# Batched matmul of transposed operands: next batch's transposes, as words of two bf16, ahead of this batch's matmuls; b loaded four rows to a partition; stores three batches behind

## The chip, the cores and the metric

The kernel runs on one core of a Trainium2 chip. The metric is the device time of one execution in microseconds (us); lower is better. A core has a matrix engine (TensorE, PE in the profile, with its weight loads listed apart as PEld), a vector engine (VectorE, DVE), a scalar engine (ScalarE, ACT), a general engine (GpSimd, POOL) and a synchronisation engine (SyncE, SP) from whose queue this kernel starts its transfers. Sixteen DMA engines move the data between the main memory and the core's working memory, which has 128 partitions. The matrix engine writes to a separate accumulator memory (PSUM).

## The reference

There are 16 independent products. Both operands arrive transposed: a is stored as k by m, b as n by k.

```python
batch, m, k, n = 16, 512, 512, 512
a: (batch, k, m) float32      b: (batch, n, k) float32
np.matmul(a.transpose(0, 2, 1), b.transpose(0, 2, 1)).astype(np.float32)
```

So `out[i][m][n]` is the sum over k of `a[i][k][m] * b[i][n][k]`. Each batch reads 1 MiB of a and 1 MiB of b and writes 1 MiB of output; over 16 batches that is 33.55 MB read and 16.78 MB written.

## The kernel before, in words

The matrix engine contracts over the partitions, so k must lie on the partitions in both operands. a has k as its rows already: partition ki takes the four rows k = 4 ki + rk (rk from 0 to 3), one run of 8 KB. b has n as its rows and must be transposed on the chip. Its view puts row n = 128 no + ni on partition ni, so that a partition takes four runs of 2 KB from four places (`b_v`, "b (no ni) k -> b ni no k").

One loop runs over the batches, and all of a batch's work stands in it in order:

- two loads from SP's queue, b first (L54), then a (L56), into pools of three buffers each;
- four casts of a to bf16 on ACT, each 128 by 512 (L60);
- for each rk, four transposes of 128 by 128 fp32 blocks on PE (L68; k is taken in steps of four elements, so that it matches a's order) into one PSUM bank, and a copy of that bank by DVE (L73) that turns it into bf16 and writes it to `bt_sb`;
- for each of four residues rm of the output rows, four matmuls of 128 by 128 by 512 that accumulate over rk in one PSUM bank (L80), and an eviction into `o_sb`, by ACT for even rm (L88) and by DVE for odd rm (L90);
- the store of the batch LAG = 6 earlier (L50, called at L93), again from SP's queue. The last six stores follow behind the loop (L96).

Each engine takes its instructions in this written order, and the waits between engines and for free buffers are put in by the tile framework. Nothing is planned apart from that. An instruction at the head of SP's queue that must wait, for a buffer to come free or for an eviction, therefore holds the transfers written behind it. There are four PSUM banks for transposes and four for outputs, and eight output buffers.

Of the kernel before, what the change touches and what calls it, by code (L numbers as in the profile page):

```python
# [1 line left out]

# [5 lines left out]


@with_exitstack
def kernel(
    ctx: ExitStack,
    tc: tile.TileContext,
    a: bass.AP,
    b: bass.AP,
    out: bass.AP,
):
    nc = tc.nc
    P = 128  # L20
    B, K, M = a.shape
    _, N, _ = b.shape
    KO = K // P
    MO = M // P
    NO = N // P

    f32 = mybir.dt.float32
    cdt = mybir.dt.bfloat16

    a_v = a.rearrange("b (ki ko) m -> b ki ko m", ko=KO)  # L30
    b_v = b.rearrange("b (no ni) k -> b ni no k", ni=P)
    out_v = out.rearrange("b (mi mo) n -> b mi mo n", mo=MO)

    const = ctx.enter_context(tc.tile_pool(name="const", bufs=1))
    identity = const.tile([P, P], f32)
    make_identity(nc, identity)

    a_pool = ctx.enter_context(tc.tile_pool(name="a_pool", bufs=3))
    b_pool = ctx.enter_context(tc.tile_pool(name="b_pool", bufs=3))
    ac_pool = ctx.enter_context(tc.tile_pool(name="ac_pool", bufs=4))  # L40
    bt_pool = ctx.enter_context(tc.tile_pool(name="bt_pool", bufs=3))
    o_pool = ctx.enter_context(tc.tile_pool(name="o_pool", bufs=8))
    psum_t = ctx.enter_context(tc.tile_pool(name="psum_t", bufs=4, space=bass.MemoryType.PSUM))
    psum_o = ctx.enter_context(tc.tile_pool(name="psum_o", bufs=4, space=bass.MemoryType.PSUM))

    LAG = 6
    o_tiles = {}

    def emit_out_dma(j):
        nc.sync.dma_start(out_v[j], o_tiles.pop(j))  # L50

    for i in range(B):
        b_sb = b_pool.tile([P, NO, K], f32)
        nc.sync.dma_start(b_sb, b_v[i])  # L54
        a_sb = a_pool.tile([P, KO, M], f32)
        nc.sync.dma_start(a_sb, a_v[i])  # L56

        a_bf = ac_pool.tile([P, KO, M], cdt)
        for rk in range(KO):
            nc.scalar.copy(a_bf[:, rk, :], a_sb[:, rk, :])  # L60
        a_br = a_bf.rearrange("p rk (pm rm) -> p rk rm pm", rm=MO)

        b_sr = b_sb.rearrange("p no (pk rk) -> p no rk pk", rk=KO)
        bt_sb = bt_pool.tile([P, KO, N], cdt)
        for rk in range(KO):
            bt_ps = psum_t.tile([P, N], f32)
            for no in range(NO):
                nc.tensor.transpose(  # L68
                    bt_ps[:, no * P:(no + 1) * P],
                    b_sr[:, no, rk, :],  # L70
                    identity,
                )
            nc.vector.tensor_copy(bt_sb[:, rk, :], bt_ps)  # L73

        o_sb = o_pool.tile([P, MO, N], f32)
        o_tiles[i] = o_sb
        for rm in range(MO):
            o_ps = psum_o.tile([P, N], f32)
            for rk in range(KO):
                nc.tensor.matmul(  # L80
                    o_ps,
                    a_br[:, rk, rm, :],
                    bt_sb[:, rk, :],
                    start=(rk == 0),
                    stop=(rk == KO - 1),
                )
            if rm % 2 == 0:
                nc.scalar.copy(o_sb[:, rm, :], o_ps)  # L88
            else:
                nc.vector.tensor_copy(o_sb[:, rm, :], o_ps)  # L90

        if i >= LAG:
            emit_out_dma(i - LAG)  # L93

    for j in range(B - LAG, B):
        emit_out_dma(j)  # L96


# [1 line left out]
_INS = ['a', 'b']  # L100
_OUTS = [((16, 512, 512), 'float32')]


# [23 lines left out]
```

## Time and profile before

| What | Before |
|---|---|
| Time, median of 3 runs (lowest to highest) | 129.46 us (129.3 to 129.65) |
| Span of the profiled execution, first to last instruction | 127.8 us |
| Profiled execution's own device time | the profile gives its span only |
| PE busy / its weight loads | 92.5 us (72%) / 60.6 us (47%) |
| DVE busy | 61.5 us (48%) |
| ACT busy | 54.8 us (43%) |
| Transfers: bytes, mean rate | 50.42 MB, 394 GB/s |
| Largest groups by busy time | matmuls 59.0 us, DVE transposed copies 40.0 us, transposes 35.7 us, ACT casts 34.9 us |
| Median time from issue to landing, 1 MiB each | b 15.4 us, a 17.3 us, out 17.4 us |

Busy shares are of the span. The page also gives the span in 40 equal slices, with one digit per slice for the busy share of each engine (9 is 90% or more), and the granted clock of the matrix engine in the same way. A matmul's listed duration includes the time in which it overlaps its neighbours, so its pace is better read from start to start. Time to landing counts from the issue on SP and includes the time that the transfer queues behind earlier ones. A timeline line gives start, duration, engine, line and operation, and in brackets the idle time before it with what ended it.

### The profile page before, as it was taken

The numbers are of one execution on the slowest core, as the hardware profiler recorded it, in microseconds if no ns is written. First come the engines' busy times: TensorE is split into PE (matmuls) and PEld (weight loads), VectorE is DVE, ScalarE is ACT, GpSimd is POOL, SyncE is SP. The second block draws the span as 40 slices with busy tenths as digits, with TensorE's granted clock in tenths as the row PEclk, the third lists the DMA queues.
The fourth block names the chain that finished last, engine by engine and source line by source line (L and its number), as shares of the span: only waits on it lengthen the run. The fifth ranks groups of instructions, "written<-read, shape, count | busy, mean of one in ns | idle before, by whom it ended". The sixth has DMA issues, their size and how long they took to land.

```text
span 127.8 us, 1405 instructions
## 1 busy us (share of the span) xinstructions
PE 92.5 (72%) x504; PEld 60.6 (47%) x512; DVE 61.5 (48%) x96; ACT 54.8 (43%) x97; POOL 0.7 (1%) x6
## 2 busy tenths in 40 slices
PE   0099999999999995768767796877779777670000
PEld 0094858678586763364634536353364634430000
DVE  0053668586774865463544727355472635640000
ACT  4026747646674635407163460816337072540000
POOL 2000000000000000000000000000000000000000
PEclk9999999999999999999999999999999999998555
DMA  3999999999999999999999999999999999999980
GB/s 90 402 370 422 406 399 420 382 409 398 404 417 415 417 419 394 416 410 429 420 410 423 406 436 405 416 426 413 427 402 431 412 424 418 426 428 428 426 346 36
DMA packets 13063, 50.42 MB, mean 394 GB/s; under 512 B 768, under 2 KB 768, under 8 KB 8960
## 3 DMA queue, kind: packets, MB, share of 16 engines
q1 hardware_dynamic: 13056, 50.33, 97.5%
q8 instruction: 4, 0.07, 0.2%
q14 instruction: 3, 0.02, 0.0%
HBM read 33.55 MB, written 16.78 MB: 394 GB/s over the span
## 4 chain that ended last, share of the span: by engine, by line
DMA 50%; PE 34%; SPq 3%; ACT 1%; issue 1%; DVE 1%; ACTq 0%
DMA a_sb<-in_a_dram 32%; PE o_ps L80 22%; DMA out_dram<-o_sb 13%; PE bt_ps L68 12%; DMA b_sb<-in_b_dram 4%; SPq L56 3%; ACT a_bf L60 1%; DVE o_sb L90 1%; ACT o_sb L88 0%; ACTq L60 0%; SPq L50 0%
## 5 line engine op out<-in xcount | busy, mean ns | idle before, releaser
L80 PE MATMUL o_ps<-bt_sb,a_bf 128*128 128x512 bf16 x248 | 59.0, 385 | 9.1 <-ACT a_bf L60 8.7
L60 ACT CAST a_bf<-a_sb 128x512 bf16<-128x512 f32 x64 | 34.9, 615 | 39.6 <-DMA a_sb<-in_a_dram 39.5
L73 DVE CAST bt_sb<-bt_ps 128x512 bf16<-128x512 f32 x64 | 40.0, 683 | 14.7 <-PE bt_ps L68 14.7
L68 PE MATMUL bt_ps<-identity,b_sb 128*128 128x128 f32 x256 | 35.7, 295 | 12.8 <-DMA b_sb<-in_b_dram 12.8
L80 PEld LDWEIGHTS <-a_bf 128*128 128x128 bf16 x256 | 27.3, 115 | 35.8 <-ACT a_bf L60 17.7
L68 PEld LDWEIGHTS bt_ps<-identity,b_sb 128*128 128x128 f32 x256 | 33.9, 211 | 17.5 <-PE o_ps L80 8.5
L90 DVE COPY o_sb<-o_ps 128x512 f32<-128x512 f32 x32 | 22.1, 692 | 38.9 <-PE o_ps L80 21.9
L88 ACT COPY o_sb<-o_ps 128x512 f32<-128x512 f32 x32 | 18.8, 586 | 19.0 <-PE o_ps L80 18.9
L60 ACT ACT_TABLE_LOAD x1 | 1.3, 1283 | 0.7 <-PEq L111 0.7
masks.py:199 POOL TENSOR_SCALAR_AFFINE_SELECT identity<-identity 128x128 f32<-128x128 f32 x1 | 0.3, 292 | 0.1
masks.py:197 POOL MEMSET identity<- 128x128 f32 x1 | 0.2, 204 | 0.3 <-POOLq L111 0.3
L111 POOL MEMSET const-bfloat16-1.0<- 128x1 bf16 x1 | 0.1, 101 | 0.0
L111 POOL MEMSET const-uint8-127<- 128x1 uint8 x1 | 0.1, 101 | 0.0
L111 POOL MEMSET const-float32-0.0<- 128x1 f32 x1 | 0.1, 98 | 0.2 <-issue 0.2
L111 POOL MEMSET const-float32-1.0<- 128x1 f32 x1 | 0.1, 98 | 0.0
## 6 DMA issues: line engine op xcount, KB each, us to landing
b_sb<-in_b_dram SPq DMA_DIRECT2D x16, 1024.0 KB, 15.4
a_sb<-in_a_dram SPq DMA_DIRECT2D x16, 1024.0 KB, 17.3
out_dram<-o_sb SPq DMA_DIRECT2D x16, 1024.0 KB, 17.4
```

What stands on the lines that cost most here:

```text
L56: nc.sync.dma_start(a_sb, a_v[i])
L60: nc.scalar.copy(a_bf[:, rk, :], a_sb[:, rk, :])
L68: nc.tensor.transpose(bt_ps[:, no * P:(no + 1) * P], b_sr[:, no, rk, :], identity,)
L73: nc.vector.tensor_copy(bt_sb[:, rk, :], bt_ps)
L80: nc.tensor.matmul(o_ps, a_br[:, rk, rm, :], bt_sb[:, rk, :], start=(rk == 0), stop=(rk == KO - 1),)
L88: nc.scalar.copy(o_sb[:, rm, :], o_ps)
L90: nc.vector.tensor_copy(o_sb[:, rm, :], o_ps)
L111: nc = _bacc.Bacc("TRN2", target_bir_lowering=False, num_devices=1)
```

## The change

- **b's layout.** Row n = 4 ni + no goes to partition ni, so a partition takes four neighbouring rows, one run of 8 KB.
- **b is cast first.** DVE casts the whole b tile of a batch to bf16 in one instruction (128 by 2048). The result is looked at as fp32 words, each of which is a pair of bf16 with neighbouring k. Eight transposes of 128 by 128 words take the place of sixteen.
- **n put in order by the copies.** The columns come out of the transposes grouped by no; two DVE copies per batch write them to word position n = 4 ni + no, that is with a step of four words. The matmuls then read one half of each word: bf16 elements with a step of two.
- **a in two casts** on ACT, each 128 by 1024, in place of four.
- **Order.** The body is split in `load`, `prepare` and `multiply`. A pass of the loop loads and prepares batch i (casts, transposes, copies), then multiplies and evicts batch i - 1, then stores batch i - 4. LAG is 3; the last three stores follow behind the loop.
- **Buffers.** a and b four each in place of three, bf16 a three in place of four, two for the bf16 b, outputs six in place of eight.

```diff
-    b_v = b.rearrange("b (no ni) k -> b ni no k", ni=P)
+    b_v = b.rearrange("b (ni no) k -> b ni no k", no=NO)
...
-    LAG = 6
+    LAG = 3
...
-        for rk in range(KO):
-            nc.scalar.copy(a_bf[:, rk, :], a_sb[:, rk, :])
...
-        b_sr = b_sb.rearrange("p no (pk rk) -> p no rk pk", rk=KO)
-        bt_sb = bt_pool.tile([P, KO, N], cdt)
-        for rk in range(KO):
-            bt_ps = psum_t.tile([P, N], f32)
+        bc = bc_pool.tile([P, NO, K], cdt, name="bc")
+        nc.vector.tensor_copy(bc, b_sb)
+        bc_w = bc.bitcast(f32).rearrange("p no (pk j) -> p no j pk", j=KJ)
+        bt_sb = bt_pool.tile([P, KJ, N], f32, name="bt_sb")
+        bt_w = bt_sb.rearrange("p j (ni no) -> p j no ni", no=NO)
+        for j in range(KJ):
+            bt_ps = psum_t.tile([P, NO, P], f32, name="bt_ps")
             for no in range(NO):
-                nc.tensor.transpose(
-                    bt_ps[:, no * P:(no + 1) * P],
-                    b_sr[:, no, rk, :],
-                    identity,
-                )
-            nc.vector.tensor_copy(bt_sb[:, rk, :], bt_ps)
+                nc.tensor.transpose(bt_ps[:, no, :], bc_w[:, no, j, :], identity)
+            nc.vector.tensor_copy(bt_w[:, j, :, :], bt_ps)
+        b_use[i] = bt_sb.bitcast(cdt).rearrange("p j (n h) -> p j h n", h=2)
...
+        for h in range(2):
+            nc.scalar.copy(a_bf[:, 2 * h:2 * h + 2, :], a_sb[:, 2 * h:2 * h + 2, :])
...
-                    bt_sb[:, rk, :],
+                    bt_h[:, rk // 2, rk % 2, :],
...
+    for i in range(B + 1):
+        if i < B:
+            load(i)
+            prepare(i)
+        if i >= 1:
+            multiply(i - 1)
+        if i >= LAG + 1:
+            nc.sync.dma_start(out_v[i - 1 - LAG], o_tiles.pop(i - 1 - LAG))
     for j in range(B - LAG, B):
-        emit_out_dma(j)
+        nc.sync.dma_start(out_v[j], o_tiles.pop(j))
```

More of the change, by code (lines that the diff above doesn't have):

```diff
@@ L23 @@
     KO = K // P
+    KJ = KO // 2
     MO = M // P
@@ L36 @@
     make_identity(nc, identity)
-    a_pool = ctx.enter_context(tc.tile_pool(name="a_pool", bufs=3))
-    b_pool = ctx.enter_context(tc.tile_pool(name="b_pool", bufs=3))
-    ac_pool = ctx.enter_context(tc.tile_pool(name="ac_pool", bufs=4))
+    a_pool = ctx.enter_context(tc.tile_pool(name="a_pool", bufs=4))
+    b_pool = ctx.enter_context(tc.tile_pool(name="b_pool", bufs=4))
+    ac_pool = ctx.enter_context(tc.tile_pool(name="ac_pool", bufs=3))
+    bc_pool = ctx.enter_context(tc.tile_pool(name="bc_pool", bufs=2))
@@ L41 @@
     bt_pool = ctx.enter_context(tc.tile_pool(name="bt_pool", bufs=3))
-    o_pool = ctx.enter_context(tc.tile_pool(name="o_pool", bufs=8))
+    o_pool = ctx.enter_context(tc.tile_pool(name="o_pool", bufs=6))
     psum_t = ctx.enter_context(tc.tile_pool(name="psum_t", bufs=4, space=bass.MemoryType.PSUM))
     psum_o = ctx.enter_context(tc.tile_pool(name="psum_o", bufs=4, space=bass.MemoryType.PSUM))
-    LAG = 6
-    o_tiles = {}
-    def emit_out_dma(j):
-        nc.sync.dma_start(out_v[j], o_tiles.pop(j))
@@ L52, with load, prepare @@
-    for i in range(B):
-        b_sb = b_pool.tile([P, NO, K], f32)
+    LAG = 3
+    o_tiles, a_tiles, b_tiles, a_use, b_use = {}, {}, {}, {}, {}
+    def load(i):
+        b_tiles[i] = b_sb = b_pool.tile([P, NO, K], f32, name="b_sb")
         nc.sync.dma_start(b_sb, b_v[i])
-        a_sb = a_pool.tile([P, KO, M], f32)
+        a_tiles[i] = a_sb = a_pool.tile([P, KO, M], f32, name="a_sb")
         nc.sync.dma_start(a_sb, a_v[i])
-        a_bf = ac_pool.tile([P, KO, M], cdt)
-        for rk in range(KO):
-            nc.scalar.copy(a_bf[:, rk, :], a_sb[:, rk, :])
-        a_br = a_bf.rearrange("p rk (pm rm) -> p rk rm pm", rm=MO)
-        b_sr = b_sb.rearrange("p no (pk rk) -> p no rk pk", rk=KO)
-        bt_sb = bt_pool.tile([P, KO, N], cdt)
-        for rk in range(KO):
-            bt_ps = psum_t.tile([P, N], f32)
-            for no in range(NO):
-                nc.tensor.transpose(
-                    bt_ps[:, no * P:(no + 1) * P],
-                    b_sr[:, no, rk, :],
-                    identity,
-                )
-            nc.vector.tensor_copy(bt_sb[:, rk, :], bt_ps)
-        o_sb = o_pool.tile([P, MO, N], f32)
-        o_tiles[i] = o_sb
+    def prepare(i):
+        b_sb, a_sb = b_tiles.pop(i), a_tiles.pop(i)
+        bc = bc_pool.tile([P, NO, K], cdt, name="bc")
[5 more added lines that the diff above has]
+            bt_ps = psum_t.tile([P, NO, P], f32, name="bt_ps")
+            for no in range(NO):
+                nc.tensor.transpose(bt_ps[:, no, :], bc_w[:, no, j, :], identity)
+            nc.vector.tensor_copy(bt_w[:, j, :, :], bt_ps)
+        b_use[i] = bt_sb.bitcast(cdt).rearrange("p j (n h) -> p j h n", h=2)
+        a_bf = ac_pool.tile([P, KO, M], cdt, name="a_bf")
+        for h in range(2):
+            nc.scalar.copy(a_bf[:, 2 * h:2 * h + 2, :], a_sb[:, 2 * h:2 * h + 2, :])
+        a_use[i] = a_bf.rearrange("p rk (pm rm) -> p rk rm pm", rm=MO)
@@ L77, with multiply @@
+    def multiply(i):
+        a_br, bt_h = a_use.pop(i), b_use.pop(i)
+        o_tiles[i] = o_sb = o_pool.tile([P, MO, N], f32, name="o_sb")
         for rm in range(MO):
-            o_ps = psum_o.tile([P, N], f32)
+            o_ps = psum_o.tile([P, N], f32, name="o_ps")
             for rk in range(KO):
@@ L90 @@
                 nc.vector.tensor_copy(o_sb[:, rm, :], o_ps)
-        if i >= LAG:
-            emit_out_dma(i - LAG)
+    for i in range(B + 1):
[6 more added lines that the diff above has]
+            nc.sync.dma_start(out_v[i - 1 - LAG], o_tiles.pop(i - 1 - LAG))
     for j in range(B - LAG, B):
-        emit_out_dma(j)
+        nc.sync.dma_start(out_v[j], o_tiles.pop(j))
 _INS = ['a', 'b']
```

## The prediction

> **What bounds the kernel now.** I read the page's slices and DMA queues first, since they say whether any engine has to be fast at all.
>
> ```profile
> PE   0099999999999995768767796877779777670000
> ...
> DMA  3999999999999999999999999999999999999980
> ...
> q1 hardware_dynamic: 13056, 50.33, 97.5%
> ```
>
> The transfer engines are full from the second slice to the last but one; no compute engine is. What counts is how long 48 transfers of 1 MiB take in one first-in-first-out queue. To split that by kind I read the timeline of ACT and PE: an a cast that waited for its load dates that load's landing, and a transpose group that waited dates b's.
>
> ```profile
> 31.09 2.18 ACT L60 CAST a_bf<-a_sb 128x512 bf16<-128x512 f32 x4 [0.90 <-DMA a_sb<-in_a_dram]
> 36.25 2.18 ACT L60 CAST a_bf<-a_sb 128x512 bf16<-128x512 f32 x4 [0.69 <-DMA a_sb<-in_a_dram]
> ...
> 100.04 2.17 PE L68 MATMUL bt_ps<-identity,b_sb 128*128 128x128 f32 x16 [0.78 <-DMA b_sb<-in_b_dram]
> 102.45 2.18 ACT L60 CAST a_bf<-a_sb 128x512 bf16<-128x512 f32 x4 [3.43 <-DMA a_sb<-in_a_dram]
> 107.58 2.17 PE L68 MATMUL bt_ps<-identity,b_sb 128*128 128x128 f32 x16 [0.77 <-DMA b_sb<-in_b_dram]
> 110.00 2.18 ACT L60 CAST a_bf<-a_sb 128x512 bf16<-128x512 f32 x4 [3.43 <-DMA a_sb<-in_a_dram]
> 110.67 3.69 PE L80 MATMUL o_ps<-bt_sb,a_bf 128*128 128x512 bf16 x15 [0.92 <-ACT a_bf L60]
> ```
>
> In the steady part a batch is one store, one b, one a: 110.00 - 102.45 = 7.55 us. An a follows its b by 110.00 - 107.58 = 2.42 us. Where only loads run, a pair takes 36.25 - 31.09 = 5.16 us, so b takes about 2.72 there. For stores I read the windows of the end, where nothing else is left (columns: stretch, us, busy of PE, its weight loads, DVE, ACT, POOL, clock, DMA share, GB/s).
>
> ```profile
> 109.92:117.00 7.08, 3.64 (x15) 1.61 (x16) 2.29 (x4) 3.35 (x6) 0.00 (x0) 1.00 1.01 428
> 117.00:122.00 5.00, 0.00 (x0) 0.00 (x0) 0.00 (x0) 0.00 (x0) 0.00 (x0) 0.54 1.00 424
> 123.50:124.00 0.50, 0.00 (x0) 0.00 (x0) 0.00 (x0) 0.00 (x0) 0.00 (x0) 0.50 0.66 279
> ```
>
> A store at 424 to 428 GB/s takes 1.0486 MB / 0.426 = 2.46 us. So b takes 7.55 - 2.42 - 2.46 = 2.67 us: 0.25 more than a for the same bytes (0.30 by the load-only stretch). The difference between the two loads is their pieces:
>
> ```profile
> DMA packets 13063, 50.42 MB, mean 394 GB/s; under 512 B 768, under 2 KB 768, under 8 KB 8960
> ```
>
> The 8960 - 768 = 8192 pieces between 2 and 8 KB are b's rows (16 x 512); a and out move in 2048 pieces of 8 KB each. The last bytes move near 124.2, the span ends 3.6 us later.
>
> [...] here the last window holds such a drop: clock 0.54 over 117 to 122 puts it near 117.4, 3.0 us after the last matmul ended at 114.37.
>
> **The change, part by part.**
>
> *b in 8 KB pieces.* b's load becomes piece for piece what a's is: 128 runs of 8 KB. Price per load falls from 2.67-2.72 to 2.42, so 16 x 0.25 to 16 x 0.30 = 4.0 to 4.8 us; I take 0.27, so 4.3 us. Nothing hides it: the queue is the bound from 2.3 us on. [...] A new batch is 2.42 + 2.42 + 2.46 = 7.30 us.
>
> *Transposes of word pairs.* 8 transposes instead of 16. They stay fp32 128x128, at 2.17 / 16 = 0.136 each: 1.09 us. [...] DVE gets a cast of 128x2048, which this trace doesn't have[...]. I take 1.23. The PSUM copies fall from 4 to 2; their write steps 16 bytes, so between 0.69 (the row of the old copy is 683 ns) and twice that. DVE per batch: 1.23 + 2 x 0.69 + 2 x 0.69 = 4.0[...]. ACT casts a in two instructions of 1024; by the old row two of 512 cost 1.23, less one fixed part, so about 1.05 each: ACT 2.1 + 2 x 0.59 = 3.3 us. All this lies beside the transfers; if that cover were gone, the cast would cost 1.23 us a batch between b's landing and its transposes, and the eight transposes saved would give back 1.09.
>
> *Matmuls on pairs.* For PE's pace I take an early stretch of its timeline, where it waits for nothing:
>
> ```profile
> 16.07 3.62 PE L80 MATMUL o_ps<-bt_sb,a_bf 128*128 128x512 bf16 x15
> 19.52 2.07 PE L68 MATMUL bt_ps<-identity,b_sb 128*128 128x128 f32 x16
> ```
>
> From start to start, 16 matmuls take 19.52 - 16.07 = 3.45 us, 0.216 each (x15: a record is missing). After the change the moving operand steps 4 bytes. [...] I take no loss; the far end, half rate, is 0.432 each. PE per batch: 1.09 + 3.45 = 4.54 of 7.30.
>
> *The order.* Matmuls of i-1 stand behind the transposes of i on PE, evictions of i-1 behind the a cast of i on ACT and the b cast of i on DVE, and the store of i-4 behind b and a of i on SP. So a store k can be issued only once batch k+1 has landed: 4.4 us after a(k+1) (see the end below). SP's next loads b(k+5), a(k+5) queue behind it; their buffers (four each) are free by then. Behind a(k+1) the queue still holds S(k-3), b, a, S(k-2), b, a, S(k-1), b, a: nine transfers, about 22 us. A wait of 4.4 us is hidden by that, and would have to grow by 17 us to starve the engines. At the start four buffers let eight loads go out where six went; the queue is full with six (no slice after the first is short), so I count nothing. The o buffers (six) are not short either: store k is through about three batches before its buffer's next use.
>
> *The end.* Here the shorter lag shows. Put 0 at the landing of a15, where b15 landed at -2.42. DVE casts until -1.1, PE transposes until 0, then runs the 16 matmuls of 14 until 3.5; ACT casts a15 until 2.1 and evicts two; DVE's last eviction of 14 ends at 4.4, store 14 goes. Matmuls of 15 follow on PE, 3.5 to 7.0, last eviction at 7.85, store 15 is issued. Bytes: landing is seen about 1.0 us after the last byte (b0's 1.05 MB were through near 5.2 and PE was released at 6.2), and first bytes follow an issue by 1.5 (0.73 to about 2.3 for b0). S11 to S14 therefore run from -1.0 to 8.8, and store 15's bytes start at 9.4: the engines idle 0.6 us, where six stores in hand left no gap before. Between 0 (all a little quicker) and 2 us[...].
>
> Sum: 127.8 - 4.3 + 0.6 = 124.1 us of span. The median of the runs is 129.46, 1.66 above this span, for what lies around it; the change touches none of that, so 129.46 - 3.7 = **125.8 us**, with 124.9 to 126.8 from the ends of the two terms.
>
> **Rivals.**
>
> *A cold PE at the end.* PE now idles 7.30 - 4.54 = 2.76 us in one piece per batch, where it had gaps of 0.8 and 0.9. The trace shows a drop 3.0 us after the last matmul. If the last batch falls in such a spell, 8 transposes take 1.8 us (the first group ran at 3.66 / 16 = 0.229) and the first matmuls 0.43 each: store 15 comes 1.4 to 3.1 us later, the gap is 2.0 to 3.7 us: 126.9 to 128.9, say 128.0. Mid-run it is hidden (even 1.8 + 5.2 is under 7.30). Against it: 2.76 is under 3.0, and no spell of the steady part, with its own gaps, shows a clock under 1.00.
>
> *Pieces matter less.* If something other than b's pieces made 2.67 us,[...] Against it: the a load beside it, same bytes, same queue.
>
> *PE becomes the bound (slower).* If a moving operand of 4-byte steps is read at half rate, a batch is 16 x 0.432 + 1.09 = 8.0 us, above 7.30. It decides from 0.39 us per matmul. Start near 7.5, 16 batches to 135.5, last eviction 0.9, store 1.5 + 2.46, end 3.6: span 144, run 145.6. No strided moving bf16 operand in the trace speaks either way[...].
>
> **How the numbers follow.** Main case 0.69, cold end 0.14, small packet gain 0.06, PE bound 0.07, and 0.04 for another loss of over 4 us, such as a starved queue. 0.3% (0.4 us) is about what a measurement of this kernel tells from no change. Faster: the main case, nearly all of the cold end and most of the small gain, 0.87; same 0.03; slower 0.10. The range reaches from 124.6 (all engines at the a load's pace, no gap) to 128.2, through most of the cold end.
>
> **What would show it.** b waits and a waits 2.4 us apart, a batch of 7.3 us; pieces under 8 KB down to 768 and GB/s slices near 425 from the start; PE near 4.5 us per batch; a dip in the DMA share one store before the end. Wrong if the matmul row grows past 0.39 us apart, if DMA digits fall mid-run, or if b still takes 2.67.

## The result, and the profile after

The change made the kernel slower: 135.4 us median of 4 runs (134.95 to 135.63) against 129.38 us (129.2 to 129.65), a ratio of 1.0468 with a 95% interval of 1.0442 to 1.0494. The profiled execution spans 133.7 us against 127.8. The forecast was 125.8 us, with a range of 124.6 to 128.2.

The page of the kernel after, slices and transfers (a digit is the busy share of one fortieth of the span, some 3.3 us):

```profile
PE   0079799998749378393893937938379383765930
...
PEclk9999999999999968999689997799977999998698
DMA  4999999999999999999999999999999999807015
GB/s 113 414 429 427 431 427 422 402 373 395 417 431 431 427 429 429 426 427 419 426 422 431 427 424 427 427 427 427 417 429 426 429 427 429 368 27 314 0 78 235
DMA packets 6918, 50.41 MB, mean 377 GB/s; under 512 B 768, under 2 KB 768, under 8 KB 768
```

The part of the change that concerns the transfers did what it says: the packets under 8 KB fell from 8960 to 768, and the rate is near 427 GB/s in most slices, where before it went between 370 and 436. But the transfer engines, which were full to the last slice but one, now run dry: 27, 0 and 78 GB/s in three of the last five slices. The loads are all done by then and the stores wait for something. Two stretches of the end (columns: stretch, us, busy of PE, its weight loads, DVE, ACT, POOL, clock, DMA share, GB/s) show for what:

```profile
112.00:120.00 8.00, 4.99 (x24) 2.75 (x24) 4.82 (x7) 3.39 (x6) 0.00 (x0) 1.00 0.61 255
...
124.00:128.00 4.00, 4.00 (x14) 1.52 (x12) 0.69 (x1) 1.17 (x2) 0.00 (x0) 0.73 0.00 0
```

From 124 to 128 nothing moves, and PE is at the last batch's matmuls. The chain that ended last is no longer made of transfers (50% before):

```profile
PE 60%; DVE 24%; issue 7%; DMA 4%; ACT 1%
```

This is one turn of that chain (start, duration, what; times in us):

```profile
44.29 1.23 DVE bc L65
...
45.65 0.73 PE bt_ps L74 x4
...
46.41 1.07 DVE bt_sb L75
...
47.52 5.41 PE o_ps L89 x16
52.95 0.04 DVE o_sb L99
52.99 0.57 issue
53.56 1.23 DVE bc L65
```

Read it against the source. The cast of b, its transposes, the copy and sixteen matmuls follow each other, and the next cast starts only when DVE's last eviction has ended (the 0.04 and 0.57 are that eviction). The matmuls at 47.52 wait for the copy that began at 46.41: they are those of the *same* batch as the transposes at 45.65, not of the batch before. Nothing of two batches overlaps on PE and DVE. A turn takes 7.68 us where the matmuls run at full clock (44.29 - 36.60 = 7.69) and 9.27 where they don't (53.56 - 44.29; the granted clock is 0.50 from 47.62 to 51.03). PE's timeline shows both (in brackets the idle time before, and what ended it):

```profile
37.97 1.20 PE L74 MATMUL bt_ps<-identity,bc 128*128 128x128 f32 x8 [2.01 <-DVE bc L65]
39.85 3.80 PE L89 MATMUL o_ps<-bt_sb,a_bf 128*128 128x512 bf16 x16 [0.68 <-DVE bt_sb L75]
45.65 1.20 PE L74 MATMUL bt_ps<-identity,bc 128*128 128x128 f32 x8 [2.01 <-DVE bc L65]
47.52 5.39 PE L89 MATMUL o_ps<-bt_sb,a_bf 128*128 128x512 bf16 x16 [0.67 <-DVE bt_sb L75]
```

The table of waits says that the data is not what is late (columns: total us, times, longest):

```profile
DVE bc L65 <- DMA b_sb<-in_b_dram: 6.1, 2, 5.7
```

The cast waited for b twice, in the first two batches. From then on b was there and DVE had not got round to it.

It did not begin so. Batches 1 to 4 look like this on PE:

```profile
21.72 3.58 PE L89 MATMUL o_ps<-bt_sb,a_bf 128*128 128x512 bf16 x15 [0.25 <-DVE bt_sb L75]
25.14 1.11 PE L74 MATMUL bt_ps<-identity,bc 128*128 128x128 f32 x8
26.08 0.39 PE L89 MATMUL o_ps<-bt_sb,a_bf 128*128 128x512 bf16 x1
26.94 3.58 PE L89 MATMUL o_ps<-bt_sb,a_bf 128*128 128x512 bf16 x15 [0.47 <-DVE bt_sb L75]
```

Here the next batch's transposes (25.14) stand ahead of the last matmul of this one (26.08), and a batch takes 26.94 - 21.72 = 5.22 us. So the program that ran is not ordered as the source is written. The description of the kernel before and the prediction said that each engine takes its instructions in the written order. That holds for the kernel before, whose lists as built agree with its source, but it is no rule: the tile framework puts each engine's instructions into an order of its own when it builds the program. In the instruction lists of the changed kernel as built, DVE gets next cast, then copies, with the evictions around them, up to batch 4; from batch 5 to 15 it gets cast, two copies, two evictions, of one and the same batch, and PE eight transposes and sixteen matmuls of one and the same batch. Eleven of sixteen batches are serial; what it costs depends on the clock as well, as the experiment with the warm PE shows. From the matmuls of batch 4 (32.16) to those of batch 15 (122.97) that is 90.8 us, 8.26 a batch, where the transfers need 7.37 (below).

### The profile page after: what moved, and what is told of

Its sections match the earlier page's. It is cut to its first block, busy times and chain, and to the rows that moved or that the text cites. A ratio compares the mean times of both kernels' runs of the same rounds, so it can differ in the third digit from the quotient of the medians.

```text
span 133.7 us, 1110 instructions
## 1 busy us (share of the span) xinstructions
PE 89.4 (67%) x384; PEld 46.8 (35%) x384; DVE 71.4 (53%) x80; ACT 50.6 (38%) x65; POOL 0.7 (1%) x6
## 4 chain that ended last, share of the span: by engine, by line
PE 60%; DVE 24%; issue 7%; DMA 4%; ACT 1%
PE o_ps L89 51%; DVE bt_sb L75 12%; DVE bc L65 11%; PE bt_ps L74 9%; DMA b_sb<-in_b_dram 4%; DVE o_sb L99 1%; ACT a_bf L80 1%; ACT o_sb L97 0%
## 5 line engine op out<-in xcount | busy, mean ns | idle before, releaser
L89 PE MATMUL o_ps<-bt_sb,a_bf 128*128 128x512 bf16 x256 | 71.1, 434 | 9.6 <-DVE bt_sb L75 8.9
L89 PEld LDWEIGHTS <-a_bf 128*128 128x128 bf16 x256 | 30.5, 120 | 45.8 <-issue 24.1
L75 DVE COPY bt_sb<-bt_ps 128x512 f32<-128x512 f32 x32 | 31.7, 1068 | 14.0 <-PE bt_ps L74 14.0
L74 PE MATMUL bt_ps<-identity,bc 128*128 128x128 f32 x128 | 19.7, 299 | 29.1 <-DVE bc L65 29.1
L80 ACT CAST a_bf<-a_sb 128x1024 bf16<-128x1024 f32 x32 | 31.9, 1047 | 9.1 <-DMA a_sb<-in_a_dram 9.1
L74 PEld LDWEIGHTS bt_ps<-identity,bc 128*128 128x128 f32 x128 | 17.6, 209 | 35.2 <-issue 34.7
L65 DVE CAST bc<-b_sb 128x2048 bf16<-128x2048 f32 x16 | 19.5, 1218 | 6.1 <-DMA b_sb<-in_b_dram 6.1
```

Source lines behind the costliest of these rows:

```text
L65: nc.vector.tensor_copy(bc, b_sb)
L74: nc.tensor.transpose(bt_ps[:, no, :], bc_w[:, no, j, :], identity)
L75: nc.vector.tensor_copy(bt_w[:, j, :, :], bt_ps)
L80: nc.scalar.copy(a_bf[:, 2 * h:2 * h + 2, :], a_sb[:, 2 * h:2 * h + 2, :])
L89: nc.tensor.matmul(o_ps, a_br[:, rk, rm, :], bt_h[:, rk // 2, rk % 2, :], start=(rk == 0), stop=(rk == KO - 1),)
```

## The experiments

Theory 1: the built order is the cause; where PE and DVE do one batch in series, the chain of 7.68 to 9.27 us is longer than its transfers. The rivals, which the expectations name: the halved clock, the copies with a step, and (theory 3) the stores only three behind, which starve the transfers by themselves. All times are medians; the kernel before, beside them on the same chip, was at 129.35 to 129.48 us.

**PE pinned to the written order.** The framework can be told to keep chosen instructions in the order of the source. Only PE's are:

```diff
-                nc.tensor.transpose(bt_ps[:, no, :], bc_w[:, no, j, :], identity)
+                tc.keep_in_program_order(nc.tensor.transpose(bt_ps[:, no, :], bc_w[:, no, j, :], identity))
...
-                nc.tensor.matmul(
+                tc.keep_in_program_order(nc.tensor.matmul(
```

> The changed kernel with PE's instructions held in the order in which they are written: transposes of batch i, then matmuls of i-1. Theory 1 (order: the framework put the matmuls of batch i right behind the transposes of the same batch, so that cast, transposes, first copy, matmuls and last eviction run one after the other, 7.68 us a batch with a warm PE and 9.27 with a cold one): the copy (1.07) drops out of the loop, cast 1.23 + transposes 1.09 + matmuls 3.45 + eviction and waits 0.9 = 6.7 us is under the transfers' 7.30, and the time is near my forecast, 125 to 128 us. Theory 2 (PE's clock drops whatever the order): cold groups stay, batches average about 8 us, 131 us or more. Theory 3 (stores three behind): no change, 135 us.

Measured: 127.03 us (126.9 to 127.19), ratio 0.981 (0.9777 to 0.9844). PE's timeline of this kernel:

```profile
47.01 1.20 PE L74 MATMUL bt_ps<-identity,bc 128*128 128x128 f32 x8 [2.01 <-DVE bc L65]
48.05 3.80 PE L89 MATMUL o_ps<-bt_sb,a_bf 128*128 128x512 bf16 x15
53.86 1.20 PE L74 MATMUL bt_ps<-identity,bc 128*128 128x128 f32 x8 [2.01 <-DVE bc L65]
```

The matmuls follow the transposes without a gap, as they are those of the batch before; a batch is 53.86 - 47.01 = 6.85 us. Only PE is held, but the lists of DVE and ACT, as built, follow it: the evictions behind the copies of batch i are now those of i-1 from the first batch to the last. So this is a test of the order as a whole and not of one engine's. Same instructions, same buffers, same lag, another order: 8.4 us. The wait of 2.01 for the cast, which is still behind the evictions on DVE, stays.

**Serial from the first batch.** Both engines pinned, and the matmuls of batch i written right behind its preparation:

```diff
-        if i >= 1:
-            multiply(i - 1)
+            multiply(i)
```

> The changed kernel with PE and DVE held in one order for all batches: cast, transposes, copies, matmuls, evictions of batch i, then those of i+1. Theory 1 (this order, which the framework chose from batch 5 on, is the cause; LAG only moves the batch from which it is chosen): all 16 batches now take the 7.68 and 9.27 us in turn, 5.6 + 16 x 8.45 + 5 = 146, about 147.5 us, slower still. Theory 3 (the stores): no more than the changed kernel's 135.4.

Measured: 149.55 us (149.53 to 149.57), ratio 1.1552 (1.1505 to 1.1599). The matmuls of batch 0 start at 9.27, those of batch 15 at 137.27: 8.53 a batch, all the way. That is 14.2 us over the changed kernel. The batches that ran ahead there account for most of it: the matmuls of batch 4 begin at 43.78 in place of 32.16, 11.6 us later. The rest comes in the eleven turns that are serial in both kernels; they take 8.50 us here and 8.26 there, with five of them slow in place of four, and in the others PE waits 0.28 us more for the second copy.

**Stores six behind.** The changed kernel with the old lag and eight output buffers:

```diff
-    LAG = 3
+    LAG = 6
```

> The changed kernel with stores six behind and eight output buffers, as before the change. Theory 1: the end is set by the last batch's eviction near 129 us and its store, so 135.4 us within 0.5. Theory 3 (the shorter lag lets the transfer engines run dry and that costs the time): 130 to 132 us.

Measured: 126.51 us (126.28 to 126.88), ratio 0.9772 (0.9735 to 0.981). Theory 1, as I had put it, failed here: it said that the lag makes no difference. PE's timeline of this kernel shows what it does:

```profile
46.46 3.80 PE L89 MATMUL o_ps<-bt_sb,a_bf 128*128 128x512 bf16 x16 [0.48 <-DVE bt_sb L75]
...
54.15 3.80 PE L89 MATMUL o_ps<-bt_sb,a_bf 128*128 128x512 bf16 x15 [0.69 <-DVE bt_sb L75]
...
61.87 5.27 PE L89 MATMUL o_ps<-bt_sb,a_bf 128*128 128x512 bf16 x16 [0.70 <-DVE bt_sb L75]
```

The matmuls of batches 1 to 7 begin 5.2 us apart, up to 46.46; in the changed kernel these ended with batch 4 at 32.16. Then the same series of 7.7 and 9.2 us sets in. Serial batches are eight, not eleven, and the last eviction starts at 117.97 in place of 128.26, 10.3 us earlier. Three batches of 5.22 in place of 8.26 are 9.1 us of that; the kernel was already 1.4 ahead at batch 4 (30.78 against 32.16). The median fell by 8.9. In both kernels the first serial batch is number LAG + 2, the first whose loads stand behind a store in SP's queue. That the framework plans with times of its own and then takes b to be later is a reading of this coincidence, not something that a run shows. Why the order turns stays open.

That leaves the question what the lag does by itself. Two kernels: the one before with stores three behind and six output buffers, and the pinned one above with six and eight.

```diff
-    LAG = 6
+    LAG = 3
```

> The kernel before with stores three behind and six output buffers, nothing else changed. Theory 1 (the shorter lag costs only through the order that the framework then builds, and the old body has no chain that is longer than its transfers): within 1.0 us of before, 129.0 to 130.5. Theory 3 (stores close behind their evictions starve the transfer queue by themselves): 132 to 135.

Measured: 129.58 us (128.96 to 130.22), ratio 1.0021 (1.0007 to 1.0036): 0.3 us.

```diff
-    LAG = 3
+    LAG = 6
```

> The changed kernel with PE pinned to the written order, as in e1_order, and stores six behind with eight output buffers in place of three and six. Theory 1 (with PE's order fixed, the lag has little left to decide): 126 to 127.2, within 1 us of e1_order's 127.0. Theory 3 (the lag matters by itself, through the transfers): 124.5 to 125.5, at the pace of the transfers.

Measured: 126.39 us (126.05 to 126.72), ratio 0.9771 (0.9741 to 0.9801); 0.64 below the pinned kernel with three. With the order held, three more batches of lag are worth 0.3 to 0.6 us, not 8.9. Theory 3 is out. The comparison can be read the other way too: with stores six behind, holding the order is worth only 0.1 us (126.39 against 126.51). Eight serial batches, behind eight that ran ahead, still end early enough for the transfers; eleven do not.

**PE kept warm.** Eight matmuls more behind each batch's own, on the operands at hand into a bank that nobody reads (one of the four transpose banks makes room):

```diff
+        if i < B - 1:
+            warm = psum_w.tile([P, N], f32, name="warm")
+            for _ in range(8):
+                tc.keep_in_program_order(nc.tensor.matmul(
+                    warm, a_br[:, 3, 3, :], bt_h[:, 1, 1, :], start=True, stop=True))
```

> The changed kernel with eight extra matmuls behind each batch's own, into a bank that nobody reads, to fill PE's idle 2.0 us; the order of the rest stays. Theory 1 with the clock as an amplifier: every batch takes the warm 7.68 us from 36.6 on, 36.6 + 11 x 7.68 = 121.1, plus about 5 for the last store, span near 126, 127.5 us. If the clock has no part in it, 135 us; if the extra matmuls delay the transposes, more than that.

Measured: 130.93 us (ratio 1.0108, 1.0065 to 1.0151); the granted clock averages 0.996 in place of 0.933. PE's timeline of this kernel:

```profile
43.72 3.80 PE L90 MATMUL o_ps<-bt_sb,a_bf 128*128 128x512 bf16 x16 [0.67 <-DVE bt_sb L76]
47.36 1.97 PE L104 MATMUL warm<-bt_sb,a_bf 128*128 128x512 bf16 x8
49.44 1.23 PE L75 MATMUL bt_ps<-identity,bc 128*128 128x128 f32 x8
51.33 3.79 PE L90 MATMUL o_ps<-bt_sb,a_bf 128*128 128x512 bf16 x15 [0.67 <-DVE bt_sb L76]
```

The extra work fills the 2.01 us in which PE waited for the cast, and every serial batch takes 7.61 us: batch 4 to batch 15, from 36.11 to 119.83, takes 83.7 us in place of 90.8. The clock is therefore worth about 7 us of the changed kernel there, plus 1.5 in its last group (5.25 us against 3.80), together 8.5. The forecast of 127.5 was missed because the extra matmuls lengthen the early batches, where PE is the bound: the matmuls of batch 4 begin at 36.11 in place of 32.16. Even warm, the serial chain is longer than the transfers, but only by 0.24 us a batch (7.61 against 7.37).

So the order and the clock have to be taken together. Without the low clock, the serial kernel would come to about 127 us: 135.4 less 8.5, or 130.93 less the 3.95 of the early batches. That is an estimate, as no run has the full clock without the extra matmuls; it is below the kernel before and level with the pinned one (127.03). The serial order by itself thus costs about 1 us beside the order of the last experiment (125.85). The rest comes through the clock, which the gaps of the serial order bring down. The low clock alone does no such harm either: the last experiment below drops to it too, in an order with several batches in work, and its transfers stay full.

**No order of n in the copies.** The two copies write in sequence; the output's columns are therefore permuted.

```diff
-        bt_w = bt_sb.rearrange("p j (ni no) -> p j no ni", no=NO)
+        bt_w = bt_sb.rearrange("p j (no ni) -> p j no ni", no=NO)
```

> The changed kernel with the two copies per batch writing side by side instead of every fourth word; this leaves the order of n out, so the output's columns are permuted. The copies should fall from 1.07 to 0.69 us. If the first copy is in the loop (theory 1), each of the 11 serial batches loses 0.38 us: about 131 us, clock dips as before. If the step costs nothing that matters, 135.4.

Measured: 127.84 us (127.32 to 128.36), ratio 0.9875 (0.9813 to 0.9936), some 3 below the forecast. The copies' rows in the groups (columns: busy us, mean ns of one, idle before) of the changed kernel, then of this one:

```profile
L75 DVE COPY bt_sb<-bt_ps 128x512 f32<-128x512 f32 x32 | 31.7, 1068 | 14.0 <-PE bt_ps L74 14.0
```

```profile
L75 DVE COPY bt_sb<-bt_ps 128x512 f32<-128x512 f32 x32 | 20.8, 686 | 14.8 <-PE bt_ps L74 14.8
```

The step costs 0.38 us a copy, and the first of the two is in the chain: a warm turn is 7.30 us in place of 7.68. The rest comes from the clock. PE waits 0.30 for the copy in place of 0.67, and only every third or so group is slow: of the groups from 46.79 to 117.29 three (54.09, 84.90, 108.39), and nine intervals average 7.83 us. By these figures a serial order with cheap copies and a full clock would have stayed just within its transfers (7.30 against 7.37); no run shows it.

**b's layout on the old body.** First alone, with n left permuted in the output:

```diff
-    b_v = b.rearrange("b (no ni) k -> b ni no k", ni=P)
+    b_v = b.rearrange("b (ni no) k -> b ni no k", no=NO)
```

> The kernel before with b loaded four rows to a partition and nothing else; n is left in the order of the transposes, so the output's columns are permuted. No instruction of PE, ACT or DVE changes. If the 8 KB runs give what I forecast, 16 x 0.27 us: 125.1 us (124.5 to 125.7). [...]

Measured: 126.35 us (126.19 to 126.4), ratio 0.9758 (0.9732 to 0.9784). ACT's timeline dates the landings of a:

```profile
84.63 2.18 ACT L60 CAST a_bf<-a_sb 128x512 bf16<-128x512 f32 x4 [3.23 <-DMA a_sb<-in_a_dram]
...
106.74 2.18 ACT L60 CAST a_bf<-a_sb 128x512 bf16<-128x512 f32 x4 [3.24 <-DMA a_sb<-in_a_dram]
```

Three batches in 22.11 us, 7.37 each, where the old body took 7.55: the large pieces are worth 0.18 us a batch, 2.9 us in all.

Then with the order of n restored by the old body's four copies, which now write bf16 elements with a step of four:

```diff
-            nc.vector.tensor_copy(bt_sb[:, rk, :], bt_ps)
+            nc.vector.tensor_copy(
+                bt_sb[:, rk, :].rearrange("p (ni no) -> p no ni", no=NO),
+                bt_ps.rearrange("p (no ni) -> p no ni", no=NO),
+            )
```

> The kernel before with b's layout alone: four rows to a partition, 8 KB runs, and n put in order by the four copies, which write bf16 with a step of four. If the transfers gain what I forecast (0.27 us a batch, 4.3 in all), 125.1 us (124.5 to 126). [...] If the stepped copies (1.07 instead of 0.69 each) make a loop of PE and DVE longer than the transfers, above 127 with transfer slices below full.

Measured: 134.31 us (ratio 1.0373, 1.0332 to 1.0413). The group of the copies in this kernel:

```profile
L73 DVE CAST bt_sb<-bt_ps 128x512 bf16<-128x512 f32 x64 | 76.0, 1327 | 6.9 <-PE bt_ps L68 6.9
```

One takes 1.33 us in the mean, where it took 0.683 before; four in a row take 4.75. Each group of matmuls waits for its copy, and from the fourth batch on the loop is 7.55 us at full clock (mean 0.995): DVE and PE set it, not the transfers. So the new layout does not come free in the old body, and the pairs as words, which need two stepped copies of 1.07 us, are the cheaper way to order n. The 125.1 of the expectation is not reached; the other case that it names came.

**Everything ahead.** The changed kernel with both engines pinned and one stage more: the cast of batch i, then transposes and copies of i-1, then matmuls of i-2; stores six behind, eight output buffers, three for the bf16 b and four for the bf16 a.

```diff
-            prepare(i)
-        if i >= 1:
-            multiply(i - 1)
-        if i >= LAG + 1:
+            cast_b(i)
+        if 1 <= i <= B:
+            prepare(i - 1)
+        if i >= 2:
+            multiply(i - 2)
+        if i >= LAG + 2:
```

> The changed kernel with an order of its own, held on PE and DVE: the cast of batch i, the transposes and copies of i-1, the matmuls of i-2; stores six behind, eight output buffers, three for bf16 b, four for bf16 a. PE then waits for nothing that the same pass makes: 4.5 us of PE and 4.6 of DVE a batch, below the transfers' 7.30, and six stores cover the end. Theory 1: transfer-bound to the end, 2.3 + 116.8 + 1 + 3.6 = 123.7 of span, 125.3 us (124.8 to 126). If something else holds the changed kernel, it stays above 127.

Measured: 125.85 us (125.65 to 126.03), ratio 0.9726 (0.9695 to 0.9757), the fastest of all, ahead of both kernels. Its page:

```profile
PEclk9999999999999999996899869999999976999555
DMA  4999999999999999999999999999999999999991
```

The transfers are the bound again, up to the last slice but one. PE still drops to the lower clock three times mid-run, and no transfer slice falls below full for it.

## Why the prediction was wrong

**Bound before, and bound after by forecast.** That the transfer queue sets the kernel before was right: alone, a cheaper b takes 3.0 us off (126.35 against 129.35).

**b in 8 KB pieces: mis-sized.** Forecast 0.27 us a batch, 4.3 in all; measured 0.18 and 2.9. A batch is 7.37 us, not 7.30. The 2.9 is below the 4.0 to 4.8 which the loads of the kernel before had given. I priced the new b like an a, at 2.42, and a store at 2.46, 4.88 together. With the layout alone changed an a still lands 2.39 us behind its b (84.63 against 82.24, where PE's transposes of that batch start), so b and store together take 4.98. Which of the two is dearer mid-run than I took it, no run says.

**Transposes, cast, copies, a's casts.** The cast takes 1.22 us in the mean; the 1.23 was my assumption, as the trace of the kernel before has no such cast. a's casts came as worked out, at 1.05 where two of half the size had taken 0.615 each. The first four transposes take 0.73 us in the chain, where half of 1.09 was worked out. The copy with a step took 1.07 us, where I took 0.69 and named up to 1.38. On the busy sums I was right that no engine comes near: DVE has 71.4 us of 133.7. That was the wrong sum. What counted was the length of a chain across two engines, and it is made of just these pieces: cast 1.23, four transposes 0.73, copy 1.07, matmuls 3.81, last eviction about 0.6, hand-overs the rest, 7.68. With my own durations (transposes 0.55, copy 0.69, matmuls 3.45), in a row, it would have been some 0.9 us shorter and under 7.30.

**Matmuls on pairs: nearly right.** I took no loss for a moving operand of bf16 with a step of two; that was my assumption, as the trace of the kernel before has no such operand. From start to start a warm matmul takes 0.227 us in place of 0.216, the median of all of them in the two traces (the line at 21.72 above gives 3.42 us for fifteen). That is 5%, 0.18 us a batch; the rival of a PE at half rate (0.432, 8.0 us a batch) is out.

**The order: the step that failed.** "Matmuls of i-1 stand behind the transposes of i on PE, evictions of i-1 behind ... the b cast of i on DVE." That holds in the source only. In batches 1 to 4 the built program still has the cast of i ahead of DVE's evictions of i-1, and the transposes of i ahead of the last matmul of i-1. From batch 5 on, all matmuls and evictions of i-1 stand ahead of the cast and the transposes of i. All that I had put "beside the transfers" is then in one row of 7.68 us with a full clock and 9.27 without, where 7.30 was the period of the forecast. Pinning PE gives back 8.4 us; pinning both with the cast ahead gives 125.85. The price of the lost cover which I named, 1.23 us for the cast less 1.09 for the transposes, was that of one edit, not of the row that forms when nothing overlaps.

**SP's queue and the lag.** That a later store does not starve the engines mid-run was right. The end gap of 0.6 was about right: 0.64 between the two pinned kernels, 0.3 on the old body. But the lag had a second effect, which I had no step for: with it the batch moves at which the order turns serial, and with that went most of the 8.9 us.

**The cold PE.** I took this rival for the end only and wrote that mid-run it is hidden. It is hidden only where batches overlap. In the serial chain it turns 7.68 us into 9.27, in four of the eleven intervals; a fifth slow group is the last one. With 8.5 us it is the larger part of the 9.6 that the forecast missed. So this part of the forecast fell with the order on which it stood. The reason that I gave against it, gaps of under 3.0 us, rested on one drop and was wrong as well: gaps of 2.01 and 0.67 us were enough. The drop near 117.4 of the kernel before, which I read as 3.0 us after the last matmul, lies at the end of a step of the grid described below, from 113.97 to 117.38, in which PE was busy for 12%.

**The chances.** The interval "from the ends of the two terms", 124.9 to 126.8, is a slip: those ends (4.8 and 0, 4.0 and 2) give 124.7 to 127.5, and the cold end's 126.9 should be 127.2. Nothing hangs on either. I left 0.04 for another large loss and 0.10 for slower at all, with no rival in which two engines do one batch in turn. The agreement of the last experiment with the forecast, a span of 123.9 against 124.1, is partly chance: b gave 1.1 us less than forecast by the spans (127.8 less 124.6, 3.2 of 4.3), six stores in hand left no gap at the end (0.6), and 0.7 us more came off against b's layout alone (124.6), which I haven't traced.

## What to carry to other kernels

A new order in the source is an order in the program only where it is pinned; before a forecast rests on "behind" or "ahead", find in the trace whose data each instruction waits for, in the early and in the late batches. Besides the busy time of each engine, add up the chain that one batch makes across engines, cast to eviction, and compare it with the period of the transfers: if it is longer, overlap is not a comfort but the whole margin. Ask also what the gaps of such a chain do to the clock: here a chain 0.3 us longer than its period cost little by itself, and most through the lower clock that its gaps brought. The cast that opens the chain can go ahead of the last batch's evictions on its engine; here that and one stage more gave 0.5 us over the pinned kernel with six stores in hand (125.85 against 126.39).

## What the runs showed of the hardware

- **Short gaps bring PE's clock down by half, and the drops stand on a grid in time.** With gaps of 2.01 and 0.67 us in a batch of 7.68 us (35% idle) every second group or so is slow, 5.39 us for sixteen matmuls in place of 3.80. With 2.01 and 0.30 in 7.30 us (32%) it was every third; with 2.01 alone in 6.85 us (29%) one group in the pinned kernel from 40 us on, behind a gap of 2.68. With the 2.01 filled by eight extra matmuls the clock averages 0.996. The clock records that the twelve traces keep show when it drops. In each run all drops start on one grid of 3.41 us, whose place differs from run to run, and mid-run each lasts one step. In the changed kernel the drops of mid-run start at 47.62, 64.68, 81.75, 98.82 and 122.71, which is five, five, five and seven steps apart, and the granted clock in each of these steps is 0.50. Of the steps at full clock in which PE was busy for less than 44%, by its matmul records, all 36 of the twelve traces are followed by a drop (eleven of them are idle steps behind the last matmul); of those above 50%, none of 319; in between, 4 of 15. In the changed kernel the steps ahead of the five drops have 38, 41, 45, 49 and 35%, and two of 44 and 48% have no drop behind them. By these traces it is not the length of one gap that decides but the idle time that falls into one step. A batch of 6.85 us is nearly two steps (6.83), so by these two figures the gap of the pinned kernel keeps its place in the grid for long, which is an estimate; how much of its full clock it owes to that place was not tested.
- **A step of two in a bf16 moving operand costs 5%.** A matmul of 128 by 512 takes 0.227 us from start to start at full clock, against 0.216 in sequence; at the clock of 0.50 it takes 0.427.
- **A step in DVE's writes costs more than forecast.** From PSUM, fp32 words with a step of 16 bytes take 1.07 us for 128 by 512 against 0.69 in sequence; bf16 with a step of 8 bytes 1.33 against 0.68.
